# Two-layer decoder on one core: every head pair's probabilities turned by VectorE and four SBUF-to-SBUF transfers, with values and scores placed in six visits a layer

## The chip, the cores and the metric

The kernel runs on one core of one Trainium2 chip. The metric is the device time of one execution in microseconds. Three runs of the kernel before gave 641.29, 641.0 and 639.86 us, median 641.0. PE is TensorE (PEld its weight loads), DVE VectorE, ACT ScalarE, POOL GpSimd and SP SyncE; POOL and SP issue the transfers (DMAs), and "q" behind a name is the engine's queue of such issues.

## The reference, cut to what matters

One sequence of 256 rows, 1024 wide, passes two layers and a last RMSNorm, all in float32. Each layer is

```
u = rmsnorm(h);  q, k, v = heads(u @ w_in)         # 16 heads of 64
h = h + merge(softmax(q k^T / 8 + bias, causal) v) @ w_o
u = rmsnorm(h);  h = h + (silu(u @ w_g) * (u @ w_u)) @ w_out   # 2816 wide
h = h + sigmoid(rmsnorm(h) @ w_gate) * (p @ w_up)
```

In layer 0 the bias is that of the forgetting attention, a difference of running sums of log-sigmoids that are a small projection of u. Layer 1 is block-sparse attention with blocks of 256 keys; with 256 rows there is one block, so it comes down to causal attention with a learned bias by distance (T5 buckets).

## The kernel before, in words

**Matmuls.** Every large product is taken in three passes of 32-bit matmuls on values split into a high and a low part: high by high, high by low, low by high (`mm3`, L94, L95, L96). Weights come through SP's queue as 512 or 540 KB blocks (`raw`, 6 buffers), ACT makes the high part (`whi`) and DVE the low one (`wlo`), and PE goes through the blocks in order. PSUM is a ring of 8 banks.

**Attention.** The 16 heads are taken as 8 pairs (0 to 7). `project` makes q and k of a pair (tile `pq`), the score matmuls go to `sp` (L546, L549, and in layer 0 a bias product, L374), DVE adds the mask or bias and takes row minima into `e` (L563), ACT takes the exponential with its row sum (L567), and the reciprocal `rc` of the sums scales it. For the product with v the scaled probabilities must be turned, so that keys lie on the partitions (`pt`). The turn is made in three ways:

- **Pairs 0 to 4**: ACT scales (`scaled`, L600), DVE turns 32 by 32 blocks within each partition group (`turn`, L607, two STREAM_TRANSPOSE of 128x384), POOL writes the 384 KB to DRAM (L619, tile `dt`), and when that has landed reads it back in four DMAs of 96 KB (L622).
- **Pair 5**: the same, but with 16 DMAs of 24 KB from SBUF to SBUF in place of the trip to DRAM (L614), ten on POOL's queue and six on SP's.
- **Pairs 6 and 7**: DVE scales (`normal`, L591), TensorE turns in 12 transposes a layer (`transposes`, L637), ACT copies from PSUM (L644).

`values` then multiplies v with the turned probabilities (L654 and L656, tile `po`), and ACT and DVE split the result into the high and low parts of `o` (L287, L288). The output projection is cut into eight parts (`wo`, 24 matmuls each, parts 0 to 7), and part n can begin once its columns of `o` are there and its weights split.

**Order.** A scheduler puts each engine's instructions in an order, held to that of the code by `issue_after`, `held` and the entries of `marks`. After the last projection PE does in each layer: scores 5 and 6 with values 1 and 2; part 0; scores 7; parts 1 and 2; values 3 with the transposes of pairs 6 and 7; part 3; values 4 and 6, 5 and 7; parts 4, 5, 6; part 7. Between these, DVE and ACT do minima, exponentials, scaling, turns, the splits of `o` and the splits of the weights. Each of those stretches in plain 32-bit matmuls between the three-pass ones is called a visit below. The tiles `e` and `turn` share 4 buffers, `pt` has 3.

Of the kernel before, what the change touches and what calls it, by code (L numbers as in the profile page):

```python
# [27 lines left out]
F32 = mybir.dt.float32  # L28
# [24 lines left out]
TURNED = ((0, 1, 2, 3, 4, 5), (0, 1, 2, 3, 4, 5))  # L53
# [22 lines left out]
def trunk(ctx: ExitStack, tc: tile.TileContext, xg, wx, xr, pt, w, cst, gf, rel, hot, rvm, out):  # L76
# [352 lines left out]
    def attention(layer, nm, mid, early, nf):  # L429
# [50 lines left out]
        qk, sm = {}, {}  # L480
# [12 lines left out]
        def project(j, a):  # L493
# [16 lines left out]
            far = [x for x in fresh if x[0] in TURNED[layer]]  # L510
            near = [x for x in fresh if x[0] not in TURNED[layer]]
# [7 lines left out]
            for x in near:  # L519
                with tc.issue_after(got.ins):  # L520
                    got = normal(*x)
# [16 lines left out]
        def scores(*js, then=()):  # L538
# [16 lines left out]
            for n, j in enumerate(js):  # L555
# [9 lines left out]
                for s in range(2):  # L565
                    for q in range(2):
                        last = nc.scalar.activation(e[:, s, sl[q]], e[:, s, sl[q]], AF.Exp, scale=-1.0,  # L567
                                                    bias=mn[:, 0, s, q:q + 1], accum_out=mn[:, 1, s, q:q + 1])
# [17 lines left out]
        def normal(j, e, mn):  # L586

            rc = inverse(j, mn)
            for q, c in enumerate((slice(0, P), slice(P, 3 * P))):
                at = e[:, :, c]  # L590
                got = nc.vector.tensor_tensor(at, at, rc[:, :, q:q + 1].to_broadcast(list(at.shape)), op=ALU.mult)  # L591
            sm[j] = e
            return got

        def scaled(j, e, mn):

            rc = inverse(j, mn)
            for s in range(2):
                for q, c in enumerate((slice(0, P), slice(P, 3 * P))):
                    nc.scalar.activation(e[:, s, c], e[:, s, c], AF.Copy, scale=rc[:, s, q:q + 1])  # L600
            return rc

        def turn(j, e):

            t = work.tile([P, 4, 3, 2, 32], F32, tag="e", bufs=4, name=f"turn{layer}_{j}")
            for s in range(2):
                nc.vector.transpose(t[:, :, :, s].rearrange("p c b x -> p b c x"),  # L607
                                    e[:, s].rearrange("p (b c x) -> p b c x", b=3, x=32))
            if j == 5:
                p = work.tile([P, 4, 3, 2, 32], F32, tag="pt", bufs=3, name=f"pt{layer}_{j}")  # L610
                for n in range(16):
                    a, i = divmod(n, 4)
                    queue = nc.sync if n % 8 in (0, 3, 6) else nc.gpsimd
                    queue.dma_start(p[32 * i:32 * i + 32, a], t[32 * a:32 * a + 32, i])  # L614
                for s in range(2):
                    pts[2 * j + s] = p[:, :, :, s].rearrange("p c b x -> p b c x")
                return
            d = dram.tile([P, 6 * P], F32, name=f"dt{layer}_{j}")
            nc.gpsimd.dma_start(d, t.rearrange("p c b s x -> p (c b s x)"))  # L619
            p = work.tile([P, 4, 3, 2, 32], F32, tag="pt", bufs=3, name=f"pt{layer}_{j}")  # L620
            for i in range(4):
                nc.gpsimd.dma_start(p[32 * i:32 * i + 32].rearrange("p c b s x -> p c (b s x)"),  # L622
                                    bass.AP(tensor=d.tensor, offset=d.offset + 192 * i,
                                            ap=[[6 * P, 32], [32 * 6 * P, 4], [1, 192]]))
            for s in range(2):
                pts[2 * j + s] = p[:, :, :, s].rearrange("p c b x -> p b c x")

        pts = {}

        def transposes(j, tag="pt"):  # L630

            e = sm.pop(j)
            for s in range(2):
                i = 2 * j + s
                pp = bank(f"pp{layer}_{i}")
                for q in range(3):
                    got = nc.tensor.transpose(pp[:, q * P:(q + 1) * P], e[:, s, q * P:(q + 1) * P], ident)  # L637
                if tag == "pt":
                    if s == 0:
# [468 lines left out]
```

## Time and profile before

| | |
|---|---|
| median of three runs | 641.0 us |
| the runs | 641.29, 641.0, 639.86 us |
| span of the profiled execution, first to last instruction | 638.6 us |
| granted clock of TensorE | 0.998 |
| PE busy | 630.3 us, 99% of the span |
| DVE, ACT, POOL busy | 71%, 59%, 7% |
| DMA | 134.87 MB, mean 211 GB/s |
| attention's tail, layer 0 and layer 1 | about 78.8 to 102, 390.4 to 414 us |

The profiled execution's own time isn't given apart from its span; against the first run of the three, 641.29 us, the span leaves 2.7 us that lie before the first and behind the last instruction, against the median 2.4 us.

A row of the timeline has the start in us from the span's start, the time from the start of the first to the end of the last of the instructions merged in it, engine, line, operation, tiles written and read, shape and count; a bracket at its end tells how long the engine had been idle just before, and what ended that. Matmuls overlap, so the start of the next row is a better end for a row of them than its own length.

### The profile page before, as it was taken

How to read it: one execution, taken by the hardware profiler on the slowest of the kernel's cores; microseconds unless marked ns; L12 is line 12 of the kernel's file. 1: busy time of each engine (PE TensorE's matmuls, PEld its weight loads, DVE VectorE, ACT ScalarE, POOL GpSimd, SP SyncE). 2: the span in 40 equal slices, each digit the busy share in tenths (PEclk: the TensorE clock that was granted, in tenths of full speed). 3: DMA queues.
4: the chain of work that ended last, by engine and by line, in shares of the span. 5: the costliest groups of instructions: out<-in, count | busy, mean ns of one | idle time of the engine just before them, and what ended most of it. 6: DMA issues, size and time to landing. Idle time of an engine off the chain costs nothing.

```text
span 638.6 us, 13183 instructions
## 1 busy us (share of the span) xinstructions
PE 630.3 (99%) x5285; PEld 608.4 (95%) x5285; DVE 454.8 (71%) x738; ACT 379.3 (59%) x657; POOL 47.6 (7%) x93
## 2 busy tenths in 40 slices
PE   9999999999999999999999999999999999999995
PEld 7899999999999999999989999899999999999985
DVE  6777888776666666659892788888666666666685
ACT  6677787654444445448664689866444444454663
POOL 0102350000000000000000034300000000000001
PEclk9999999999999999999999999999999999999999
DMA  8846987497766666566674579756766666666523
GB/s 337 318 141 210 261 235 264 133 339 262 236 201 197 196 198 214 184 200 198 190 245 164 185 260 264 236 190 211 211 193 197 199 201 199 194 204 190 191 92 107
DMA packets 41469, 134.87 MB, mean 211 GB/s; under 512 B 5408, under 2 KB 10432, under 8 KB 41408
## 3 DMA queue, kind: packets, MB, share of 16 engines
q1 hardware_dynamic: 37616, 125.05, 60.9%
q0 software_dynamic: 3360, 8.36, 4.6%
q8 instruction: 41, 0.67, 0.4%
q10 hardware_dynamic: 432, 0.62, 0.3%
q14 instruction: 20, 0.16, 0.1%
HBM read 127.17 MB, written 9.20 MB: 214 GB/s over the span
## 4 chain that ended last, share of the span: by engine, by line
PE 95%; ACT 1%; DMA 1%; DVE 1%; issue 1%; POOL 0%; SPq 0%; POOLq 0%; DVEq 0%; ACTq 0%
PE gu L94 13%; PE gu L95 13%; PE gu L96 13%; PE fo L96 6%; PE fo L95 6%; PE fo L94 6%; PE pq L94 5%; PE pq L95 5%; PE pq L96 5%; PE v L425 4%; PE wo L94 2%; PE wo L96 2%; PE wo L95 2%; PE pg L94 2%; PE pg L95 2%; PE pg L96 2%
## 5 line engine op out<-in xcount | busy, mean ns | idle before, releaser
L168 DVE TENSOR_TENSOR wlo<-raw,whi 128x1024 fp32r<-128x1024 f32 (+1 forms) x166 | 200.8, 1216 | 76.4 <-ACT whi L166 70.7
L166 ACT ACTIVATE whi<-raw 128x1024 fp32r<-128x1024 f32 x164 | 171.9, 1058 | 104.6 <-issue 51.2
L94 PE MATMUL gu<-g,whi 128*128 128x256 f32 x704 | 194.9, 277 | 0.0
L95 PE MATMUL gu<-g,whi 128*128 128x256 f32 x704 | 194.7, 277 | 0.0
L96 PE MATMUL gu<-g,wlo 128*128 128x256 f32 x704 | 194.5, 276 | 0.0
L96 PEld LDWEIGHTS gu<-g,wlo 128*128 128x128 f32 x704 | 132.3, 188 | 0.0
L95 PEld LDWEIGHTS gu<-g,whi 128*128 128x128 f32 x704 | 132.2, 188 | 0.1
L94 PEld LDWEIGHTS gu<-g,whi 128*128 128x128 f32 x704 | 132.2, 188 | 0.0
L96 PE MATMUL fo<-fp,wlo 128*128 128x256 f32 x352 | 97.4, 277 | 0.0
L94 PE MATMUL fo<-fp,whi 128*128 128x256 f32 x352 | 97.3, 276 | 0.0
L95 PE MATMUL fo<-fp,whi 128*128 128x256 f32 x352 | 97.3, 276 | 0.0
L185 DVE TENSOR_TENSOR wlo<-raw,whi 128x1080 fp32r<-128x1080 f32 x40 | 50.9, 1279 | 29.5 <-ACT whi L184 28.9
L94 PE MATMUL pq<-g,whi 128*128 128x256 f32 x256 | 71.4, 279 | 0.0
L95 PE MATMUL pq<-g,whi 128*128 128x256 f32 x256 | 70.8, 276 | 0.0
L96 PE MATMUL pq<-g,wlo 128*128 128x256 f32 x256 | 70.8, 276 | 0.0
L95 PEld LDWEIGHTS fo<-fp,whi 128*128 128x128 f32 x352 | 66.2, 188 | 0.0
L94 PEld LDWEIGHTS fo<-fp,whi 128*128 128x128 f32 x352 | 66.1, 188 | 0.0
L96 PEld LDWEIGHTS fo<-fp,wlo 128*128 128x128 f32 x352 | 66.1, 188 | 0.0
L184 ACT ACTIVATE whi<-raw 128x1080 fp32r<-128x1080 f32 x40 | 43.7, 1101 | 27.6 <-PE gu L95 27.1
L94 PEld LDWEIGHTS pq<-g,whi 128*128 128x128 f32 x256 | 48.1, 188 | 0.9
L95 PEld LDWEIGHTS pq<-g,whi 128*128 128x128 f32 x256 | 48.1, 188 | 0.1
L96 PEld LDWEIGHTS pq<-g,wlo 128*128 128x128 f32 x256 | 48.1, 188 | 0.0
(189 smaller groups left out, 1023.8 us busy)
## 6 DMA issues: line engine op xcount, KB each, us to landing
raw<-w SPq DMA_DIRECT2D x173, 512.0 KB, 4.0
raw<-w SPq DMA_DIRECT2D x40, 540.0 KB, 4.0
dt<-turn POOLq DMA_DIRECT2D x10, 384.0 KB, 4.1
pt<-dt POOLq DMA_DIRECT2D x40, 96.0 KB, 5.5
d<-d SPq DMA_DIRECT2D x4, 768.0 KB, 6.4
bias<-d SPq DMA_DIRECT2D x4, 512.0 KB, 6.3
dh<-end SPq DMA_DIRECT2D x2, 512.0 KB, 2.6
ut<-dh SPq DMA_DIRECT2D x8, 128.0 KB, 3.0
```

The costliest lines, as they stand in the source:

```text
L94: mm(o, ah, bh, start=start, stop=False, skip_group_check=True)
L95: mm(o, ah, bl, start=False, stop=False, skip_group_check=True)
L96: return mm(o, al, bh, start=False, stop=stop, skip_group_check=True)
L166: state["hi"] = state[f"hi{i}"] = nc.scalar.activation(hi[:, c], raw[:, c], AF.Copy)
L168: nc.vector.tensor_tensor(lo[:, c], raw[:, c], f32(hi[:, c]), op=ALU.subtract)
L184: nc.scalar.activation(ht, raw[:, 0:WW], AF.Copy)
L185: state["lo"] = nc.vector.tensor_tensor(lt, raw[:, 0:WW], f32(ht), op=ALU.subtract)
L425: got = mm(bks[2 * t + hf], x[a][:, t * P:(t + 1) * P], w[b][:, hf * HC:(hf + 1) * HC], start=k + a + b == 0, stop=k + b == KT, skip_group ...
```

## The change

`TURNED`, the trip to DRAM, the 16 small DMAs, `transposes` and its copies go. All eight pairs are turned by `turn`: DVE's two STREAM_TRANSPOSE now read `e` with a stride of four elements (in 32-element runs that take every fourth key), so that a 32-partition group of the result holds, for one group of 32 queries, all 128 keys of a block, and four DMAs of 96 KB each take such a group from SBUF to its place in `pt` in SBUF. Their destination is 128 partitions by 192 elements, 768 bytes in a run. For pairs 0 to 4 all four are on POOL's queue; for pairs 5, 6 and 7 two are on POOL's and two on SP's. `pt` has 5 buffers. Pair 6 is now scaled by ACT; pair 7 still by DVE (`normal`), and then turned. The values of pair 3 and the scores of pair 7 join the first visit, and the order after the projections is: scores 5 and 6, values 1, 2 and 3, scores 7; parts 0, 1, 2; values 4 and 5; parts 3, 4; values 6 and 7; parts 5, 6; part 7. The scratch that POOL's queue keeps its descriptors in is set to 8192 bytes of a partition.

```diff
-                if j < NP - 3:
+                if j < NP - 3 or j == NP - 1:
                     fresh.append((j, e, mn))
-                elif j in TURNED[layer]:
+                else:
                     scaled(j, e, mn)
                     fresh.append((j, e))
-                else:
-                    marks[-j] = last, normal(j, e, mn)
...
         def turn(j, e):
             t = work.tile([P, 4, 3, 2, 32], F32, tag="e", bufs=4, name=f"turn{layer}_{j}")
             for s in range(2):
-                nc.vector.transpose(t[:, :, :, s].rearrange("p c b x -> p b c x"),
-                                    e[:, s].rearrange("p (b c x) -> p b c x", b=3, x=32))
-            if j == 5:
...
-            d = dram.tile([P, 6 * P], F32, name=f"dt{layer}_{j}")
-            nc.gpsimd.dma_start(d, t.rearrange("p c b s x -> p (c b s x)"))
-            p = work.tile([P, 4, 3, 2, 32], F32, tag="pt", bufs=3, name=f"pt{layer}_{j}")
-            for i in range(4):
-                nc.gpsimd.dma_start(p[32 * i:32 * i + 32].rearrange("p c b s x -> p c (b s x)"),
-                                    bass.AP(tensor=d.tensor, offset=d.offset + 192 * i,
-                                            ap=[[6 * P, 32], [32 * 6 * P, 4], [1, 192]]))
+                got = nc.vector.transpose(t[:, :, :, s].rearrange("p c b x -> p b c x"),
+                                          e[:, s].rearrange("p (b y c) -> p b c y", b=3, c=4))
+            p = work.tile([P, 4, 3, 2, 32], F32, tag="pt", bufs=5, name=f"pt{layer}_{j}")
+            for a in range(4):
+                queue = nc.sync if j > 4 and a % 2 else nc.gpsimd
+                queue.dma_start(p[:, a].rearrange("p b s x -> p (b s x)"),
+                                t[32 * a:32 * a + 32].rearrange("p c b s x -> p (c b s x)"))
...
-            got = scores(*range(max(j - 1, 0), min(j + 1, NP - 1)), then=(1, 2) if j == 6 else ())
+            got = scores(*range(max(j - 1, 0), min(j + 1, NP - 1)), then=(1, 2, 3) if j == 6 else ())
...
+        with tc.issue_after(got.ins):
+            got = scores(NP - 1)
+        marks["mid"] = marks[7][0], marks["low"]
         got = behind(got, 6, 0)
         fetch(1, "t")
+        with tc.issue_after(state["lo"].ins):
+            turn(*fresh.pop(0))
         fetch(2, "mid")
+        turn(*fresh.pop(0))
+        fetch(3, "mid")
+        x = fresh.pop(0)
+        normal(*x)
+        marks["third"] = (turn(*x[:2]),)
+        got = behind(got, "t", 1)
         got = behind(got, "mid", 2)
         with tc.issue_after(got.ins):
-            values(3)
-            marks["third"] = marks["o"]
-            transposes(NP - 2, "fp")
-            got = transposes(NP - 1, "fp" if far else "pt")
-        got = behind(got, -6, 3)
+            got = values(4, 5)
+            marks["o4"] = marks["o"]
+        got = behind(got, "mid", 3)
+        got = behind(got, "third", 4)
         with tc.issue_after(got.ins):
-            values(4, 6 if far else 5)
-            got = values(5 if far else 6, 7)
-        got = behind(got, "third", 4)
-        behind(got, "third", 5, 6)
+            got = values(6, 7)
+        behind(got, "o4", 5, 6)
...
-    nc = bacc.Bacc("TRN2", target_bir_lowering=False, num_devices=1)
+    nc = bacc.Bacc("TRN2", target_bir_lowering=False, num_devices=1, dynamic_dma_scratch_size=8192)
```

Three places show how the order moves. In the names a number behind the pair's is the tile's own (`po_3_1106` is `po` of pair 3); `sp_14` and `sp_15` are the two heads of pair 7. The lines are those of the kernel that the rows come from.

The first is PE's first visit of layer 0, behind scores 5 and 6. Before:

```order
L654 MATMUL po_1_1114<-pt_1_791,v 64x256 x2
L654 MATMUL po_2_1115<-pt_2_801,v 64x256 x2
L656 MATMUL po_1_1114<-pt_1_791,v 64x128 x2
L656 MATMUL po_2_1115<-pt_2_801,v 64x128 x2
L94 MATMUL wo_0_0_1158<-o_369,whi_1163 128x256
```

Now:

```order
L616 MATMUL po_1_1104<-pt_1_787,v 64x256 x2
L616 MATMUL po_2_1105<-pt_2_795,v 64x256 x2
L616 MATMUL po_3_1106<-pt_3_1000,v 64x256 x2
L618 MATMUL po_1_1104<-pt_1_787,v 64x128 x2
L618 MATMUL po_2_1105<-pt_2_795,v 64x128 x2
L618 MATMUL po_3_1106<-pt_3_1000,v 64x128 x2
L373 MATMUL sp_14_1161<-c,sel 128x384
```

PE reads `pt` of pair 3 before it does any part of the output projection, where before it came three parts later; scores 7 stand right behind.

The second is POOL's row of DMA issues in layer 0. Before:

```order
L619 DMA dt_3_1006<-turn_3_1003 128x768
L619 DMA dt_4_1016<-turn_4_1013 128x768
L622 DMA pt_3_1008<-dt_3_1006 32x4x192 x4
L622 DMA pt_4_1018<-dt_4_1016 32x4x192 x4
L614 DMA pt_5_1207<-turn_5_1204 32x192 x10
```

Now:

```order
L602 DMA pt_3_1000<-turn_3_997 128x1x192 x4
L602 DMA pt_4_1008<-turn_4_1005 128x1x192 x4
L602 DMA pt_5_1222<-turn_5_1219 128x1x192 x2
L602 DMA pt_6_1236<-turn_6_1233 128x1x192 x2
L602 DMA pt_7_1254<-turn_7_1251 128x1x192 x2
```

One step from `turn` to `pt` where there were two, each with its own landing.

The third is DVE's tail in layer 1, from the first half of pair 5's turn to that of pair 7 (`wlo_5158` and `wlo_5172` are the low weights of parts 2 and 3):

```order
L597 STREAM_TRANSPOSE turn_5_5148<-e_5_5055 128x3x4x32
L184 TENSOR_TENSOR wlo_5158<-raw_5156,whi_5157 128x1080
L576 RECIPROCAL rc_6_5081<-mn_6_5072 128x4
L597 STREAM_TRANSPOSE turn_5_5148<-e_5_5055 128x3x4x32
L184 TENSOR_TENSOR wlo_5172<-raw_5170,whi_5171 128x1080
L597 STREAM_TRANSPOSE turn_6_5162<-e_6_5071 128x3x4x32 x2
L576 RECIPROCAL rc_7_5176<-mn_7_5102 128x4
L584 TENSOR_TENSOR e_7_5101<-e_7_5101,rc_7_5176 128x2x128
L584 TENSOR_TENSOR e_7_5101<-e_7_5101,rc_7_5176 128x2x256
L597 STREAM_TRANSPOSE turn_7_5180<-e_7_5101 128x3x4x32 x2
```

Before, the two halves of pair 5's turn stood together behind part 2's low weights, and there was none for pairs 6 and 7. Now part 2's low weights stand between the halves of pair 5's turn. On SP's queue the two DMAs of `pt_5` stand behind the issue of the weights `raw_5440`.

More of the change, by code (lines that the diff above doesn't have):

```diff
@@ L479, in attention @@
         oh, ol = o[:, :, 0], o[:, :, 1]
-        qk, sm = {}, {}
+        qk = {}
         pq = {}
@@ L509, in project @@
             del pq[j]
-            far = [x for x in fresh if x[0] in TURNED[layer]]
-            near = [x for x in fresh if x[0] not in TURNED[layer]]
+            far = fresh[:]
             fresh.clear()
@@ L518, in project @@
             marks["t"] = marks.get(j - 1, (got,))[0], got
-            for x in near:
-                with tc.issue_after(got.ins):
-                    got = normal(*x)
             th = work.tile([P, 3 * P], F32R, tag="qkh", bufs=3, name=f"qkh{layer}_{j}")
@@ L590, in normal @@
                 at = e[:, :, c]
-                got = nc.vector.tensor_tensor(at, at, rc[:, :, q:q + 1].to_broadcast(list(at.shape)), op=ALU.mult)
-            sm[j] = e
-            return got
+                nc.vector.tensor_tensor(at, at, rc[:, :, q:q + 1].to_broadcast(list(at.shape)), op=ALU.mult)
         def scaled(j, e, mn):
@@ L628, in attention @@
+            return got
         pts = {}
[L630 to L639, printed above, removed]
-                        both = work.tile([P, 2, 3 * P], F32, tag="pt", bufs=3, name=f"pt{layer}_{j}")
-                    t = both[:, s]
-                else:
-                    t = work.tile([P, 2 * S], F32, tag="fp", bufs=4, name=f"pt{layer}_{i}")[:, 0:3 * P]
-                nc.scalar.activation(t, pp[:, 0:3 * P], AF.Copy)
-                pts[i] = t.rearrange("p (b c x) -> p b c x", b=3, x=32)
-            return got
@@ L692, in behind @@
             return got
+        with tc.issue_after(got.ins):
+            got = scores(NP - 1)
+        marks["mid"] = marks[7][0], marks["low"]
         got = behind(got, 6, 0)
-        far = 5 in TURNED[layer]
-        marks["mid"] = marks[7][0], marks["low"] if far else marks[-5][1]
         fetch(1, "t")
+        with tc.issue_after(state["lo"].ins):
+            turn(*fresh.pop(0))
         fetch(2, "mid")
-        if far:
-            with tc.issue_after(state["lo"].ins):
-                turn(*fresh.pop())
-        with tc.issue_after(got.ins):
-            end = scores(NP - 1)
-        got = behind(end, "t", 1)
-        if not far:
-            with tc.issue_after(got.ins):
-                got = transposes(5, "fp")
+        turn(*fresh.pop(0))
[4 more added lines that the diff above has]
+        got = behind(got, "t", 1)
         got = behind(got, "mid", 2)
         with tc.issue_after(got.ins):
-            values(3)
-            marks["third"] = marks["o"]
-            transposes(NP - 2, "fp")
-            got = transposes(NP - 1, "fp" if far else "pt")
-        got = behind(got, -6, 3)
+            got = values(4, 5)
+            marks["o4"] = marks["o"]
+        got = behind(got, "mid", 3)
+        got = behind(got, "third", 4)
         with tc.issue_after(got.ins):
-            values(4, 6 if far else 5)
-            got = values(5 if far else 6, 7)
-        got = behind(got, "third", 4)
-        behind(got, "third", 5, 6)
+            got = values(6, 7)
+        behind(got, "o4", 5, 6)
         state["o"] = marks["o"]
@@ L722, in attention @@
             if hf:
-                wo(7, "third")
+                wo(7, "o4")
             for b in range(2):
```

16 lines of the change are left out of this document (3 added, 13 removed).

## The prediction

> **What bounds the kernel now.** I read the page first, then the list of what PE waited for, then the timelines of PE, POOL, DVE and ACT in the tail of attention in each layer, since the diff touches nothing else.
>
> ```profile
> span 638.6 us, 13183 instructions
> PE 630.3 (99%) x5285; PEld 608.4 (95%) x5285; DVE 454.8 (71%) x738; ACT 379.3 (59%) x657; POOL 47.6 (7%) x93
> PE cold L111 <- PEq L1100: 0.8, 1, 0.8
> PE po L654 <- ACT o L287: 0.6, 1, 0.6
> ```
>
> PE is busy for 99% of the span and the list of its waits has two entries, 0.8 us at the start and 0.6 us at the end of layer 1's attention. So time is gained only by taking work from PE or that one wait, and every new wait of PE is paid in full. DVE, ACT and POOL matter only where they make PE wait.
>
> **What leaves PE.** The rows of layer 0's tail, then of layer 1's:
>
> ```profile
> 84.69 0.28 PE L95 MATMUL wo<-o,whi 128*128 128x256 f32 x1
> 84.81 0.28 PE L96 MATMUL wo<-o,wlo 128*128 128x256 f32 x1
> 85.02 0.44 PE L374 MATMUL sp<-c,sel 64*128 64x384 f32 x2
> ...
> 85.97 0.39 PE L94 MATMUL wo<-o,whi 128*128 128x256 f32 x1
> 86.19 0.28 PE L95 MATMUL wo<-o,whi 128*128 128x256 f32 x1
> ...
> 91.65 0.65 PE L654 MATMUL po<-pt,v 128*64 128x256 f32 x4
> 92.13 0.39 PE L656 MATMUL po<-pt,v 128*64 128x128 f32 x4
> 92.45 1.56 PE L637 MATMUL pp<-con,e 128*128 128x128 f32 x12
> 93.77 0.37 PE L94 MATMUL wo<-o,whi 128*128 128x256 f32 x1
> ```
>
> ```profile
> 402.60 0.65 PE L654 MATMUL po<-pt,v 128*64 128x256 f32 x4
> 403.09 0.39 PE L656 MATMUL po<-pt,v 128*64 128x128 f32 x4
> 403.40 1.56 PE L637 MATMUL pp<-con,e 128*128 128x128 f32 x12
> 404.72 0.37 PE L94 MATMUL wo<-o,whi 128*128 128x256 f32 x1
> ...
> 409.72 1.08 PE L654 MATMUL po<-pt,v 128*64 128x256 f32 x8 [0.56 <-ACT o L287]
> ```
>
> The 12 transposes take 93.77 - 92.45 = 1.32 us, and 404.72 - 403.40 = 1.32 in layer 1: 2.64 together. Three-pass matmuls follow each other every 0.12 us (84.69 to 84.81). Into a visit the step is 85.02 - 84.81 = 0.21, out of it 86.19 - 85.97 = 0.22, so each visit costs about 0.2 beside its contents. Behind the projections a layer has four visits now and three after the change: 0.2 a layer, 0.4 together. The 0.56 us wait of layer 1 stands in the middle of a visit of four pairs, for the copies of the two before; the change splits it in two of two pairs with two parts between, so I let it go. Saved: 2.64 + 0.4 + 0.56 = 3.6 us.
>
> **What is late next: pair 3.** PE now wants `pt` of pair 3 in the first visit. When it wants it, and when the turned pair was ready:
>
> ```profile
> 80.55 1.08 PE L654 MATMUL po<-pt,v 128*64 128x256 f32 x8
> 81.46 0.61 PE L656 MATMUL po<-pt,v 128*64 128x128 f32 x8
> 82.00 0.38 PE L94 MATMUL wo<-o,whi 128*128 128x256 f32 x1
> 392.65 0.61 PE L656 MATMUL po<-pt,v 128*64 128x128 f32 x8
> 393.19 0.39 PE L94 MATMUL wo<-o,whi 128*128 128x256 f32 x1
> ```
>
> ```profile
> 76.12 1.95 DVE L607 STREAM_TRANSPOSE turn<-e 128x384 f32<-128x384 f32 x4
> 77.44 0.56 POOL L619 DMA_DIRECT2D dt<-turn  x1 [6.08 <-DVE turn L607]
> 81.78 2.21 POOL L622 DMA_DIRECT2D pt<-dt  x4 [2.86 <-DMA dt<-turn]
> 389.68 0.56 POOL L619 DMA_DIRECT2D dt<-turn  x1 [5.06 <-DVE turn L607]
> ```
>
> The third pair's first matmuls take the place in which L656 begins now: 81.46 in layer 0, 392.65 in layer 1. POOL begins the first transfer of pair 3 at 77.44 and 389.68; one issue takes 2.21 / 4 = 0.55, so the fourth begins 1.65 later, at 79.09 and 391.33. PE waits if that one lands more than 2.37 us (81.46 - 79.09) behind its issue in layer 0, more than 1.32 in layer 1. No transfer of 96 KB from SBUF to SBUF is in the trace. The nearest rows are POOL's reads of 96 KB from DRAM. The first pair of lines is those issued from 397 to 398 us, the second those from 81.7 to 83.6:
>
> ```profile
> L622 POOL DMA_DIRECT2D pt<-dt x3: 550/552/552, 396.5 to 397.6; - x3
> DMA to landing us min/median/max: 2.5/2.8/3.7
> ...
> DMA to landing us min/median/max: 5.7/5.8/6.2
> ```
>
> ```profile
> 79.24 2.06 SPq L151 DMA_DIRECT2D raw<-w  x2
> 391.48 2.17 SPq L151 DMA_DIRECT2D raw<-w  x2
> ```
>
> The slow ones were issued behind two 512 KB weight blocks (79.24 and the next); the quick ones had none issued beside them for 3 us. Pair 3's four transfers are nearer to the quick: the next weight blocks are issued at 79.24 and 391.48, each just behind the fourth. I take the quick rows' median, 2.8, and keep 2.5 and 5.8 for the range. In layer 0 the wait is 79.09 + 2.8 - 81.46 = 0.43 us, in layer 1 391.33 + 2.8 - 392.65 = 1.48.
>
> [...]
>
> **What is late after that: pair 5 in layer 1.** Its chain runs over ACT's scaling, DVE's turn and, between the two halves of the turn, part 2's low weights:
>
> ```profile
> 390.10 1.04 ACT L136 ACTIVATE whi<-raw 128x1024 fp32r<-128x1024 f32 x1
> 394.92 0.64 ACT L287 ACTIVATE o<-po 128x256 fp32r<-128x256 f32 x2
> 397.20 1.49 ACT L600 ACTIVATE e<-e,rc 128x128 f32<-128x128 f32 x4
> 396.87 1.28 DVE L185 TENSOR_TENSOR wlo<-raw,whi 128x1080 fp32r<-128x1080 f32 x1
> 398.06 1.24 DVE L607 STREAM_TRANSPOSE turn<-e 128x384 f32<-128x384 f32 x2
> ```
>
> ACT now has one high weight more ahead of this scaling (about 1.0) and the split of pair 3's `o` (0.64 / 2 = 0.32), so it begins near 397.20 + 1.3 = 398.5, and its first half is done 0.7 later, at 399.2. DVE then takes 1.95 / 4 = 0.49 for a half turn, 398.06 - 396.87 = 1.19 for the low weights, 0.49 for the other half: 401.4. POOL and SP begin 0.25 later and each issues its second after 0.55: 402.2. Transfers of this place, 24 KB each, and PE's parts:
>
> ```profile
> L614 SPq DMA_DIRECT2D pt<-turn x5: 533/584/593, 399.4 to 401.9; - x5
> DMA to landing us min/median/max: 3.3/3.8/4.4
> ...
> 395.92 0.28 PE L96 MATMUL wo<-o,wlo 128*128 128x256 f32 x1
> 396.12 0.49 PE L546 MATMUL sp<-qkt 64*128 64x128 f32 x4
> 396.90 0.39 PE L94 MATMUL wo<-o,whi 128*128 128x256 f32 x1
> ```
>
> At 3.8 us pair 5 lands at 406.0. PE, undisturbed, would want it at 393.19 + 0.80 (values 3, 402.60 to 403.40) + 0.78 (scores 7, 396.12 to 396.90) + 8.39 (three parts of 395.92 - 393.19 = 2.73, and 0.2 for the visit) + 0.45 (half the 0.91 of eight L654) = 403.6; with the 1.48 of pair 3, 405.1. I count 0.9 us, between nothing (landing in 2.5: 404.7) and 1.5 (in 4.4: 406.6 less 405.1).
>
> **What stays hidden.** Pair 5 in layer 0: ACT's scaling there starts 1.3 later too, and both half turns stand together; that gives 92.7 for the landing against 93.0 for PE. A landing 0.6 us later would cost 0.3. Pair 7: its turn uses the buffer of pair 5's, so DVE waits until that has landed (406.0); 1.0 for the turn, 0.8 to the second issue and 3.8 bring 411.6, where PE, by 1.45 for the visit of two pairs (80.55 to 82.00) and two parts, wants it at 403.6 + 1.45 + 5.7 + 2.4 of waits = 413.1. Behind that waiting turn stand the low weights of part 4, wanted at the same time or later; the cover is 1.5 us and goes if pair 5 lands later than that. DVE's share of new work is two turns (1.95) less one `normal`, about 1.0 a layer; ACT gains 1.5 of scaling and loses four copies. They are paid from idle time:
>
> ```profile
> sum 63.00, PE 62.44 PEld 57.63 DVE 53.70 ACT 51.69 POOL 20.89; mean PE 31.22 PEld 28.82 DVE 26.85 ACT 25.84 POOL 10.44
> ```
>
> In the two tails together (73 to 105, 385 to 416 us) DVE is idle for 9.3 us and ACT for 11.3. The smaller descriptor scratch changes nothing that a row shows; I cost it at nothing.
>
> **The sum.** -3.6 + 0.43 + 1.48 + 0.9 = -0.8 us, so a span of 637.8. The profiled span leaves 2.4 us to the median of the runs, 641.0; with the same 2.4 I expect 640.2 us. About half of the saving of layer 0 stays, and layer 1 gives its own back: 1.32 + 0.2 + 0.56 = 2.1 against 2.4 of waits.
>
> **Rivals.**
>
> *The transfers land fast.* With 2.5 us, the quickest 96 KB row, the waits are 0.13 + 1.18 and pair 5 is hidden: -3.6 + 1.3 = -2.3, or 638.7 us. For it: nothing of the weights is issued while pair 3's transfers are, and both their ends lie in SBUF. Against it: the whole 384 KB of pair 3 took 3.7 us to land in layer 0 and 4.1 in layer 1, as the views of `dt` give it:
>
> ```profile
> DMA to landing us min/median/max: 3.7/3.7/3.7
> DMA to landing us min/median/max: 4.1/4.1/4.1
> ```
>
> Less the 1.65 of the three earlier issues that leaves 2.1 and 2.4 for the same bytes, so layer 0's would allow it and layer 1's be nearer to it than to my 2.8.
>
> *The strided turn runs at half rate.* DVE now reads every fourth element. No row of this kernel shows such a read. Doubling a half turn adds 0.49, a pair's turn 0.97. Pair 3 would be ready 0.97 later in both layers and PE would wait so much longer; pair 5's chain moves by as much as PE, so its term stays. -0.8 + 1.9 = +1.1: 642.1 us. [...] Against it: the turn now moves 384 elements a partition in 0.49 us, 1.3 ns an element, a pace at which a read may still keep up.
>
> *Slower than before: the transfers queue with the weights.* If the fourth one shares the DMA engines with the 512 KB issued 0.15 us behind it, it lands in 4 to 5.8 us, as the POOL reads from 81.78 on did. At 4.8: 79.09 + 4.8 - 81.46 = 2.4 and 3.5, pair 5 then hidden behind the longer wait: -3.6 + 5.9 = +2.3, or 643.3 us. This decides from a landing of about 3.7 us on, where the two waits, 1.33 and 2.37, take back the saving. For it: the four reads of the same size from the same queue; against it: those were issued behind the weights, these ahead.
>
> **How the numbers follow.** My forecast, 640.2, has a chance of 0.45 (landing between 2.6 and 3.7 us, 639.2 to 641.8), the fast landing 0.24, the half-rate turn 0.12, the queueing 0.19. A measurement of this kernel tells 0.2%, about 1.3 us, from no change: 639.7 and 642.3 are the bounds. Faster takes the fast landing and a third of the forecast: 0.39. Within: the other two thirds and half of the half-rate case, 0.37. Slower: the queueing and the other half, 0.24. The range goes from 638.0 (the fast landing's 638.7, less the 0.13 + 0.5 that a landing half a microsecond quicker than any row would save) to 643.3, the queueing's middle.
>
> **What would show it.** In the profile after: no L637; PE's list of waits with `po` released by DMA `pt<-turn`, about 0.4 us near 81.5 and 1.5 near 392.7 (right), none (fast landing), over 2 each (queueing); a third such wait of some 0.9 near 405. The group of STREAM_TRANSPOSE with a mean near 538 ns (right) or near 1000 (half rate). The landing of `pt<-turn` in the table of issues, 2.8 (right), 2.5 or less, over 4. I am wrong if PE waits for weights or for PSUM in the tail, which nothing here foresees.

## The result and the profile after

The changed kernel takes 648.4 us (median of four runs, 647.9 to 648.8). Its ratio to the kernel before is 1.0118, with an interval from 1.0105 to 1.0132: it is slower by 1.2%, where 640.2 was forecast and the range ended at 643.3. The span of the profiled execution grew from 638.6 to 646.1 us, by 7.5. One execution of a later experiment, c_mid3, took 787.7 us at a granted clock of 0.85 and is not in its ratio; without it the median given there, 643.97, is 643.6.

From the page of the changed kernel: the busy times. Then what PE waited for in attention, where the same list had one entry of 0.6 us before:

```profile
PE 632.5 (98%) x5261; PEld 610.1 (94%) x5261; DVE 465.2 (72%) x742; ACT 378.5 (59%) x657; POOL 38.3 (6%) x75
```

```profile
PE po L616 <- DMA pt<-turn: 5.5, 2, 3.5
```

Two things stand out. The two waits of the forecast are there, at the right place and from the right releaser, and nothing else there waits; but they have 5.5 us, not 1.9. And PE executes 24 matmuls fewer than before, yet its busy time rose by 2.2 us (630.3 to 632.5).

The time can be put in a ledger by layer. The first and the last row of each layer's tail of attention, from the first scores behind the projections to the first `gu` matmul, in PE's timeline before:

```profile
78.84 0.44 PE L374 MATMUL sp<-c,sel 64*128 64x384 f32 x2
110.48 0.28 PE L94 MATMUL gu<-g,whi 128*128 128x256 f32 x1
390.38 0.49 PE L546 MATMUL sp<-qkt 64*128 64x128 f32 x3
422.18 0.28 PE L94 MATMUL gu<-g,whi 128*128 128x256 f32 x1
```

and after:

```profile
78.94 0.44 PE L373 MATMUL sp<-c,sel 64*128 64x384 f32 x2
112.89 0.28 PE L93 MATMUL gu<-g,whi 128*128 128x256 f32 x1
392.80 0.38 PE L541 MATMUL sp<-qkt 64*128 64x128 f32 x2
429.24 0.28 PE L93 MATMUL gu<-g,whi 128*128 128x256 f32 x1
```

Layer 0's tail went from 31.64 to 33.95 us, layer 1's from 31.80 to 36.44: +2.31 and +4.64, together 6.95 of the 7.5. What happened in them starts in the first visit. PE's timeline of the changed kernel, layer 0 and layer 1:

```profile
80.64 1.08 PE L616 MATMUL po<-pt,v 128*64 128x256 f32 x8
83.71 0.92 PE L616 MATMUL po<-pt,v 128*64 128x256 f32 x4 [1.99 <-DMA pt<-turn]
84.35 1.56 PE L618 MATMUL po<-pt,v 128*64 128x128 f32 x12
87.48 0.39 PE L93 MATMUL wo<-o,whi 128*128 128x256 f32 x1
...
394.16 1.08 PE L616 MATMUL po<-pt,v 128*64 128x256 f32 x8
398.77 1.12 PE L616 MATMUL po<-pt,v 128*64 128x256 f32 x4 [3.53 <-DMA pt<-turn]
412.05 0.44 PE L616 MATMUL po<-pt,v 128*64 128x256 f32 x2
```

The values of pairs 1 and 2 take 0.91 us from step to step (80.55 to 81.46 in the rows of before), so those of pair 3 could have begun at 81.55 and 395.07. They begin 2.16 and 3.70 us later: 5.9 us. Then the matmuls behind the wait are slow: the twelve of L618 take 1.56 us, and the same twelve take 0.85 in a_contig below. The reason stands in the column of the granted clock. The views of stretches of 1 us, of the changed kernel; the columns are the stretch, its length, busy time of PE, PEld, DVE, ACT and POOL, the granted clock, the share of the DMA engines, GB/s:

```profile
83.00:84.00 1.00, 0.29 (x4) 0.28 (x6) 1.00 (x3) 1.00 (x2) 0.80 (x2) 0.98 0.92 165
84.00:85.00 1.00, 1.00 (x11) 0.88 (x9) 1.00 (x8) 1.00 (x2) 0.00 (x0) 0.50 0.87 347
...
87.00:88.00 1.00, 1.00 (x10) 0.82 (x9) 0.99 (x3) 1.00 (x4) 0.00 (x0) 0.81 0.32 129
...
397.00:398.00 1.00, 0.00 (x0) 0.00 (x0) 1.00 (x3) 0.52 (x2) 1.00 (x3) 0.99 0.80 198
398.00:399.00 1.00, 0.23 (x2) 0.26 (x4) 1.00 (x2) 1.00 (x3) 0.81 (x2) 0.50 1.06 191
...
404.00:405.00 1.00, 1.00 (x7) 1.00 (x7) 0.88 (x4) 1.00 (x5) 0.00 (x0) 0.59 0.00 0
```

Half the clock is granted from 84 to about 87.4 and from 398 to about 404.8. It also explains why PE is busier with less work. Its price is found beside two of the experiments below, which do the same matmuls at full clock: 83.71 to 87.48 is 3.77 us here and 2.18 in a_contig, so 1.6; 398.77 to 412.05 is 13.28 here and 10.46 in c_light, so 2.8. The ledger of the tails is then: waits 5.9, half clock 4.4, and what is left, 6.95 - 5.9 - 4.4 = -3.3, is the work saved. Of the rest of the 7.5, about 0.1 us lies ahead of layer 0's tail and 0.45 behind layer 1's.

Why is pair 3 late? The pieces of the chain of waits of the changed kernel (start, length, what), in layer 0 and in layer 1:

```profile
77.54 1.65 DVE turn L597 x2
...
79.47 1.37 POOL pt L602 x3
...
81.06 2.52 DMA pt<-turn
...
394.48 1.37 POOL pt L602 x3
...
396.06 2.52 DMA pt<-turn
```

The last of the four transfers, the unknown of the forecast, took 2.52 us, quicker than the 2.8 taken. But POOL begins at 79.47 and 394.48 instead of 77.44 and 389.68. Against the first values of the visit (80.55 and 391.74 before, the latter 0.91 ahead of the 392.65 of L656; 80.64 and 394.16 now) that is 1.94 us and 2.38 us later. The group of the turn, before and after (count, busy us, mean ns):

```profile
L607 DVE STREAM_TRANSPOSE turn<-e 128x384 f32<-128x384 f32 x24 | 12.2, 551 | 0.2
```

```profile
L597 DVE STREAM_TRANSPOSE turn<-e 128x384 f32<-128x384 f32 x32 | 26.0, 862 | 0.2
```

A half turn that reads every fourth element takes 862 ns, 1.6 times the 551 of before, 0.31 us more, and from one start to the next 0.82 instead of 0.49. Pair 3's own two halves account for 0.6 of the delay. The rest was there already when its turn began, at 77.54 instead of 76.12, 1.4 us later: six half turns of pairs 0 to 2 stand ahead of it in the layer, and at 0.31 us each they make 1.9. DVE was idle at times in the projections. Most of that is one entry in its list of waits from 48 to 78 us, here of the changed kernel,

```profile
DVE qkl L523 <- ACT qkh L521: 3.5, 5, 1.1
```

which is the time that ACT needs to answer DVE's own instruction before. It is 3.5 us in the kernel before as well: a DVE that comes later asks later, so this idle time takes nothing of the delay away. Only one wait for PE (0.35 us behind the first pair's turn in the timeline of before) was used up.

### The profile page after: what moved, and what is told of

Read it like the earlier page. It is cut to its first block, busy times and chain, and to the rows that moved or that the text cites. A ratio compares the mean times of both kernels' runs of the same rounds, so it can differ in the third digit from the quotient of the medians.

```text
span 646.1 us, 13133 instructions
## 1 busy us (share of the span) xinstructions
PE 632.5 (98%) x5261; PEld 610.1 (94%) x5261; DVE 465.2 (72%) x742; ACT 378.5 (59%) x657; POOL 38.3 (6%) x75
## 4 chain that ended last, share of the span: by engine, by line
PE 84%; ACT 5%; DVE 5%; issue 2%; DMA 2%; POOL 1%; SPq 0%; DVEq 0%; POOLq 0%; ACTq 0%
PE gu L93 12%; PE gu L94 12%; PE gu L95 12%; PE fo L95 6%; PE fo L94 6%; PE fo L93 6%; PE v L424 4%; PE wo L93 3%; ACT e L562 2%; PE wo L94 2%; PE wo L95 2%; DVE turn L597 2%; PE pg L93 2%; PE pg L94 1%; PE pg L95 1%
```

## The experiments

Each ran beside the kernel before on the same chip, and each ratio is to that. The suspects are the strided turn (theory 1 in the expectations), the early place of pair 3's values (2), the half clock behind a wait (3), and the transfers of pair 3 beside the weights (4). Where the turn reads contiguously, `pt` holds the keys in another order than `v`, so the products are other numbers of the same shape and work.

**The change with a contiguous turn** (a_contig).

```
-  e[:, s].rearrange("p (b y c) -> p b c y", b=3, c=4)
+  e[:, s].rearrange("p (b c x) -> p b c x", b=3, x=32)
```

> The changed kernel, with the turn reading in order again (no stride of four elements), all else as changed. The keys of a block then reach TensorE in another order than v's rows, so the attention's values are other numbers; the work and its order are the same. Theory 1 (the strided read makes VectorE late, and through it TensorE): a half turn falls from 0.79 to 0.48 us apart, the wait for pair 3 from 1.99 to about 0.1 us in layer 0 and from 3.53 to about 1.1 us in layer 1, no wait for pair 5 or under 1 us in layer 1: 638.5 to 640.5 us. Theory 2 (pair 3 is wanted too early, whatever the turn takes): both waits stay over 1.5 us, 645 us or more.

646.97 us, ratio 1.0091 [1.0075, 1.0106]. The turn is back at 0.55 us a half, and POOL begins where the prediction had it, but almost nothing is won. Pieces of its chain in layer 0, then SP's row of weight issues, and the same row of the changed kernel:

```profile
76.05 1.04 DVE turn L597 x2
...
77.37 1.37 POOL pt L602 x3
...
78.95 5.03 DMA pt<-turn
```

```profile
79.17 2.06 SPq L150 DMA_DIRECT2D raw<-w  x2
```

```profile
81.84 2.06 SPq L150 DMA_DIRECT2D raw<-w  x2
```

The transfers, 2.1 us earlier in issue, land later: at 83.98, where the strided kernel's landed at 81.06 + 2.52 = 83.58. Two weight blocks of 512 KB are issued from 0.2 us behind the last transfer on, where the strided kernel issued them 0.8 behind. In layer 1, with the weights again just behind, the last took 4.7. So the stride is a cause, but not the only one. PE's visit shows the price at full clock, since here layer 0 keeps it:

```profile
84.12 0.65 PE L616 MATMUL po<-pt,v 128*64 128x256 f32 x4 [2.53 <-DMA pt<-turn]
...
86.30 0.39 PE L93 MATMUL wo<-o,whi 128*128 128x256 f32 x1
```

That is the 2.18 us of the ledger. Layer 1 waited 3.4 us and had half the clock again. So both waits stayed over 1.5 us, as theory 2 said, and the times of theory 1 did not come.

**The change with pair 3's values in the second visit** (a_late), the strided turn kept.

```
-  then=(1, 2, 3) if j == 6
+  then=(1, 2) if j == 6
...
-  got = values(4, 5)
+  got = values(3, 4, 5)
```

> The changed kernel with its strided turn, but the values of pair 3 taken from the first visit and put into the second, with those of pairs 4 and 5. Theory 2 (only the early place of pair 3 is wrong): no wait is left, 648.4 less 5.5 of waits and 5.4 of slow matmuls behind them, 637.5 us. Theory 1 (VectorE is late for everything): the wait moves to the second visit, where pair 5 lands about 2.4 us late in layer 0 and 3 to 4 in layer 1: 644 to 648 us.

649.11 us, ratio 1.0123 [1.0107, 1.014]: as slow as the change, and far from the 637.5 of theory 2. The first entries of PE's list of waits:

```profile
PE sp L541 <- DVE qkt L514: 1.8, 1, 1.8
PE wo L94 <- DVE o L287: 1.7, 2, 1.4
```

The wait for `pt` is gone from the first visit, and PE waits instead for the queries and keys of pair 7 (1.4 us more for `qkl`), the splits of `o` and the low weights, all of them DVE's; the wait for pair 5 that theory 1 had is only 0.5 us. Layer 1 ran at half clock from 401.1 to 404.5. With values 3 out of the way scores 7 come earlier, so this run moved two things. It does show that DVE is late in other work there, not in the turn alone.

**The kernel before with the strided read** (b_stride): nothing but that line.

```
-  e[:, s].rearrange("p (b c x) -> p b c x", b=3, x=32)
+  e[:, s].rearrange("p (b y c) -> p b c y", b=3, c=4)
```

> The kernel before, with nothing changed but the read of the turn, strided as in the change; the keys reach TensorE in another order than v's rows, so the attention's values are other numbers. Theory 1: VectorE is 1.4 us late at pair 3's turn in layer 0 and 2 us at pair 5's, and more in layer 1, which pair 7's scaling hands on to the transposes: a wait of TensorE of 1 to 3 us in each layer, 643 to 648 us. Theory 2 (the stride is harmless, the place of pair 3 is what costs): 641 us as before.

646.8 us, ratio 1.0095 [1.008, 1.011]. Without the new order, the new transfers or the new turns, the stride costs the kernel before some 6 us, within what theory 1 gave. Its turn in layer 0, which began at 76.12 and took 1.95 us for four halves before, and its first wait of PE:

```profile
77.61 3.16 DVE L607 STREAM_TRANSPOSE turn<-e 128x384 f32<-128x384 f32 x4
```

```profile
PE wo L94 <- DVE mn L563: 2.2, 2, 1.2
```

The clock stayed at 1.00 in both tails, so none of it is half clock. The list names 3.3 us more than before; the rest of the 6.2 in span is not explained.

**The kernel before with the new path** (b_path): pairs 0 to 5 go by four transfers from SBUF to SBUF, contiguous turn, old order.

```
-  nc.gpsimd.dma_start(d, t.rearrange("p c b s x -> p (c b s x)"))
-  for i in range(4): nc.gpsimd.dma_start(p[32 * i:32 * i + 32]..., <d, 192 * i>)
+  for a in range(4):
+      queue = nc.sync if j > 4 and a % 2 else nc.gpsimd
+      queue.dma_start(p[:, a]..., t[32 * a:32 * a + 32]...)
```

> The kernel before with one part of the change alone: pairs 0 to 5 go from the turn, which reads in order, to their place by four transfers within SBUF, no trip to DRAM; order, TensorE's transposes of pairs 6 and 7 and ScalarE's copies as before. The values of these pairs are other numbers, since the keys reach TensorE in another order. Theory 6 (the transfers themselves cost TensorE nothing where nothing waits for them early): 640 to 642 us, no wait of TensorE beyond the 0.6 us of before. Rival (the transfers disturb the weights or the engines): waits for weights, 643 us or more.

640.46 us, ratio 0.9997 [0.9987, 1.0006]. The one new wait is 0.2 us. The path alone costs nothing and brings nothing in the old order, where `pt` is read later.

**Pair 3's odd transfers on SP's queue** (c_sp, with the contiguous turn).

```
-  queue = nc.sync if j > 4 and a % 2 else nc.gpsimd
+  queue = nc.sync if j not in (0, 1, 2, 4) and a % 2 else nc.gpsimd
```

> The kernel a_contig (the changed one with the turn reading in order, values in another key order), with two of pair 3's four transfers on SP's queue, as pairs 5 to 7 have it, so that the last is issued about 1.1 us earlier, ahead of the weight block that SP issues at 79.17 us. Theory 4 (the transfers of pair 3 are slow only where they share the DMA engines with a 512 KB weight block): all four land within 2.6 us of their issue, no wait for pair 3 in layer 0, under 0.6 us in layer 1, 637.5 to 640 us. Rival (four SBUF-to-SBUF transfers in a row are slow in themselves, or while VectorE works): the last still lands over 3.7 us behind its issue, waits over 1 us, 643 us or more.

643.67 us, ratio 1.0043 [1.0028, 1.0058], with two waits left:

```profile
82.62 0.65 PE L616 MATMUL po<-pt,v 128*64 128x256 f32 x4 [1.05 <-DMA pt<-turn]
395.08 0.65 PE L616 MATMUL po<-pt,v 128*64 128x256 f32 x4 [1.98 <-DMA pt<-turn]
```

Two queues issue the four sooner, and SP's two stand ahead of the weights; it wins nearly half of a_contig's loss. But they did not land within 2.6 us, as theory 4 had it. SP's second, issued at 77.79 and 390.40, 1.4 us ahead of the weights, still took 4.70 and 4.55 us, over the 3.7 of the rival, and the time is the rival's too:

```profile
77.79 4.70 DMA pt<-turn
```

So the distance to the weights doesn't decide by itself how long a transfer takes. Layer 1's wait of 1.98 us still halved the clock, from 396.2 to 399.6.

**The weight block beside pair 3's transfers cut to a sixteenth** (c_light, contiguous turn). In each layer one block of 512 KB is loaded only in its first 64 columns and split from these repeated; the rest of its values are left out.

```
+  n = 64 if i in (30, 138) else c.stop
+  state["row"] = queue.dma_start(raw[:, c.start:n], w[max(i - 2, 0)][:, c.start:n])
```

> The kernel a_contig with 15/16 of one weight block left out in each layer (32 KB in place of 512 KB, its matmuls use those numbers again): the block that SP issues 0.2 us behind pair 3's fourth transfer, at 79.2 us and in layer 1 at 393.3. Theory 4 (that block is what makes pair 3's transfers land after 3.7 to 5.0 us): all four land within 2.7 us, the wait falls from 2.53 to 0.2 us or none in layer 0 and from 3.37 to about 1 in layer 1. Rival (they are slow among themselves, eight transfers of 96 KB in a row): the last still lands over 3.7 us behind its issue and the wait stays over 1.5 us in layer 0.

641.62 us (eight runs), ratio 1.0017 [1.0006, 1.0027]. Against the kernel before in their own sessions c_light loses 641.62 - 640.73 = 0.89 us and a_contig 646.97 - 641.22 = 5.75, so one block in each layer was worth 4.9 of the 5.75, the half clock of a_contig's layer 1 included. PE's timeline:

```profile
83.42 0.65 PE L623 MATMUL po<-pt,v 128*64 128x256 f32 x4 [0.98 <-DMA pt<-turn]
395.11 0.65 PE L623 MATMUL po<-pt,v 128*64 128x256 f32 x4 [1.23 <-DMA pt<-turn]
405.57 0.44 PE L623 MATMUL po<-pt,v 128*64 128x256 f32 x2
407.21 0.65 PE L623 MATMUL po<-pt,v 128*64 128x256 f32 x4 [0.99 <-DMA pt<-turn]
```

In layer 1 the last transfer of pair 3 now lands in 2.6 us, not 4.7, and the wait is near the 1 of theory 4. In layer 0 it lands in 3.48, not 5.03, and the wait of 0.98 lies between theory 4 and its rival. The other block of 512 KB, issued at 81.75, does not account for that: the second of the four, issued at 78.8, takes 3.9 us in this kernel as in a_contig, and it would have landed before 81.75 at the 2.5 us of layer 1. What slows layer 0's transfers beside the block that was cut stays open. The clock stayed at 1.00, and 395.11 to 405.57 is the 10.46 us of the ledger. Of all runs this one is nearest to the change as it was forecast, with a contiguous turn, landings of 3.48 and 2.6 us against 2.8, and pair 5 waiting in layer 1, and even it is no faster than the kernel before.

**Pair 3's values and scores 7 one part later** (c_mid, contiguous turn).

```
-  then=(1, 2, 3) if j == 6
+  then=(1, 2) if j == 6
...
+  got = behind(got, 6, 0)
-  got = scores(NP - 1)
+  got = scores(NP - 1, then=(3,))
-  got = behind(got, 6, 0)
```

> The kernel a_contig with pair 3's values and pair 7's scores taken one part of the output projection later (scores 5 and 6, values 1 and 2; part 0; scores 7 and values 3; parts 1, 2 and on as changed): one visit more a layer, 0.2 us each. Pair 3 is wanted 2.9 us later. Theory 5 (all that is wrong, once the turn reads in order, is that pair 3 is wanted before its transfers can be there): no wait in layer 0, under 1 us in layer 1, the granted clock stays at 1.0, 638 to 640.5 us. Rival (pairs 5 to 7 are late as well, by ScalarE's and VectorE's longer tail): waits of over 1 us move to the later visits, 642 us or more.

643.81 us, ratio 1.005 [1.0033, 1.0067], as the rival had it. PE no longer waits for pair 3, but for others:

```profile
PE wo L95 <- DVE wlo L184: 2.6, 2, 1.6
...
PE po L616 <- DMA pt<-turn: 0.7, 1, 0.7
```

Two kernels then let the low weights go earlier: **c_mid2** those of parts 2 and 3, **c_mid3** those of part 2 alone.

```
+  marks["mid"] = marks[7][0], marks["low"]     (c_mid2: set before scores 7)
```

```
+  marks["two"] = marks[7][0], marks["low"]     (c_mid3: set before scores 7)
-  fetch(2, "mid")
+  fetch(2, "two")
```

> The kernel c_mid (turn in order; pair 3's values and pair 7's scores one part later) with the low weights of parts 2 and 3 no longer held back until pair 7's minima: VectorE does them in the time in which c_mid has it idle (84.3 to 88.2 us). If the waits that are left in c_mid (2.6 us for low weights, 0.7 for pair 5) are an order on VectorE and no lack of time, the first go and 638.5 to 640.5 us come out. If VectorE and ScalarE have too much to do in the tail, the waits move to pair 5 or 7: 641.5 to 644 us.

> The kernel c_mid (turn in order, values in another key order; pair 3's values and pair 7's scores one part later) with part 2's low weights alone taken from behind pair 5's turn, part 3's left there. Theory 7 (what is left over in c_mid and c_mid2 is one order on VectorE, either weights or pair 5 first): no wait of over 0.5 us in the two tails, the 3.0 us that the transposes and the removed wait of layer 1 are worth are seen, 638 to 639.5 us. Rival (with TensorE 3 us quicker the tail is bound by VectorE, ScalarE and the transfers together, and a wait is only moved): waits of 2 us or more again, at pair 5 or at part 3's weights, 640.5 to 643 us.

644.28 us, ratio 1.0053 [1.0036, 1.0071], and 643.97 us, 1.005 [1.0033, 1.0068]: no gain from either, and both a little above what even the rivals gave. The longest wait in c_mid3:

```profile
PE po L616 <- DMA pt<-turn: 2.3, 1, 2.3
```

The wait for low weights became two for pair 5, this one in layer 1 and one of 1.5 for its turn in layer 0, where the turn now stands behind those low weights on DVE; c_mid2 has the same two (1.9 and 1.4) in its profiled execution, which at 642.04 us is the fastest of its six. In these three kernels the place of the wait was chosen, and the sum did not get smaller (3.3, 3.3 and 4.1 us).

**c_mid2's order with the strided turn** (s_mid2), the whole computation in one of these orders.

> The same order as c_mid2, but with the strided turn of the change, so that all of the computation is done. Theory 1 (the strided read makes VectorE 1.4 us late at pair 3's turn in layer 0 and 0.3 more with each turn's half): 2 to 4 us above c_mid2, 641 to 645 us. Rival (in this order VectorE has the time): within 1 us of c_mid2.

650.46 us, ratio 1.017 [1.0144, 1.0196], 6 us behind c_mid2, where theory 1 had 2 to 4. That is as much as the stride costs in b_stride, but here a part of it is half clock, from 413.6 to 417.0.

**The stride moved elsewhere.** The keys have to be interleaved by someone. In **a_wr** DVE's minimum writes the scores in the turned order, and in **x6_mid3** (c_mid3's order) ACT scales into another buffer in that order; the turn then reads contiguously, in a_wr in two pieces a half.

```
+  nc.vector.tensor_tensor_reduce(e[:, s, sl[q]].rearrange("p (c m) -> p m c", c=4), ...)      (a_wr)
```

```
+  nc.scalar.activation(x[:, s, c].rearrange("p (b c y) -> p b y c", c=4, y=32), ...)         (x6_mid3)
```

> The changed kernel with the stride moved: VectorE writes the scores' differences in the order that the turn needs (a stride in its output), and the turn reads in order; all of the computation is done. If a strided write costs VectorE nothing, it is a_contig: 645.5 to 647.5 us, minima at 0.28 and 0.42 us as before. If it costs as a strided read does (1.6 times), the minima take 0.45 and 0.68 and the chain behind them is late: 648 us or more.

> The order of c_mid3 with all of the computation done and no stride on VectorE: ScalarE's scaling of every pair, pair 7's too, writes a second tile in the order that the turn needs (6 buffers shared by e, the scaled tile and turn, 4 for pt, 7168 bytes of descriptors). If ScalarE writes with a stride at its usual pace (0.39 and 0.49 us for 128 and 256 columns), VectorE is on time as in c_mid3 and pair 7's scaling is moved from VectorE: within 1.5 us of c_mid3, at or under 641 us. If the strided write costs ScalarE as it costs VectorE (1.4 to 1.6 times), its scaling takes 0.6 us more a pair and 643 us or more come out.

647.91 us, ratio 1.0101 [1.0068, 1.0134], and 652.77 us, 1.0184 [1.0167, 1.0201]. The groups by shape, DVE's minimum before and in a_wr:

```profile
L563 DVE CUSTOM_DVE_ANT_0 e<-sp,con 128x256 f32<-128x256 f32 x16 | 6.7, 418 | 0.0
```

```profile
L558 DVE CUSTOM_DVE_ANT_0 e<-sp,con 128x256 f32<-128x256 f32 x16 | 10.0, 626 | 0.0
```

and ACT's scaling before and in x6_mid3:

```profile
L600 ACT ACTIVATE e<-e,rc 128x256 f32<-128x256 f32 x24 | 11.9, 497 | 0.0
```

```profile
L593 ACT ACTIVATE x<-e,rc 128x256 f32<-128x256 f32 x32 | 23.7, 742 | 0.0
```

The strided write cost each of the two engines 1.5 times the contiguous one, 626 ns against 418 and 742 against 497. Neither engine took the interleaving for nothing, and PE still waits for `pt`, 4.8 us in a_wr and 6.9 in x6_mid3, with half clock at both waits in each. x6_mid3 also moves other work, so its time is not the price of the write alone.

**Filling the wait** (a_fill, a_fill2): the change itself, with dummy matmuls between pair 2 and pair 3 to keep PE busy, so that only the clock differs.

```
+  if js == (1, 2, 3) and i == 4:
+      for _ in range(FILL[layer]): mm(po[d, :S], v[...], ...)      (a_fill: 17, 30; a_fill2: 5, 8)
```

> The changed kernel with 17 (layer 0) and 30 (layer 1) more matmuls ahead of those of pair 3 in the first visit, on pair 2's operands and into the bank that pair 3's overwrite: 1.95 and 3.45 us of work at 0.115 us each in the place of the wait. Theory 3 (the lower granted clock behind the wait costs 1.9 and 3.6 us beyond the wait itself): the granted clock stays near 1.0 in both tails, 643 us. Rival (the matmuls behind the wait are slow because VectorE and ScalarE are then at work on the same memory): they stay slow, 648 us.

> The changed kernel with 5 (layer 0) and 8 (layer 1) more pairs of matmuls ahead of those of pair 3 in the first visit, at the 0.43 us apiece that a_fill showed: 2.1 and 3.4 us of work in the place of the waits of 1.99 and 3.53. Theory 3 (the half clock behind the waits costs 1.9 and 3.6 us by itself): granted clock 1.0 in both tails, 642.5 to 644 us. Rival (the matmuls behind are slow for another reason): 648 us.

a_fill overshot: 659.3 us, ratio 1.0291 [1.0275, 1.0306], since a dummy (two matmuls) took 0.43 us and not the 0.115 assumed, so the fill lasted 7 and 13 us. a_fill2 took 651.3 us, 1.0163 [1.0148, 1.0178]. Its visit in layer 0, and its first wait of PE:

```profile
81.46 2.32 PE L619 MATMUL po<-pt,v 128*64 128x256 f32 x10
83.75 0.65 PE L621 MATMUL po<-pt,v 128*64 128x256 f32 x4
...
84.99 0.45 PE L374 MATMUL sp<-c,sel 64*128 64x384 f32 x2
```

```profile
PE wo L94 <- DVE o L288: 3.4, 2, 2.0
```

Pair 3 begins at the same time as in the change (83.75 against 83.71) and the clock stays at 1.00 in both tails, where it falls to 0.50 behind the change's 1.99 and 3.53 us of idle time, so it is PE's idle time that takes the clock, as theory 3 said. But PE, 0.9 us sooner at scores 7 (84.99, where the change has 85.84), now waits for DVE, and ACT's order had shifted too (the splits of `o` behind pair 5's scaling), so the time does not isolate the price of the half clock: I expected this kernel to be quicker than the change, and it is 2.9 us slower.

## Why the prediction was wrong

**What leaves PE: right, but for one term.** Without waits and half clock the tails are 3.3 us shorter by the ledger, against 3.6. The twelve transposes and layer 1's wait make 2.64 + 0.56 = 3.2 of that; the four tenths for fewer visits came to 0.1 or so. Part of why is in the rows of layer 0: the last visits of two pairs take 1.45 and 1.56 us after (95.89 to 97.34, 103.05 to 104.61), where the one of four pairs took 2.75 before (96.69 to 99.44), so splitting it cost 0.26.

**"What is late next: pair 3": the right wait, priced by the wrong term. This step failed first.** The whole uncertainty went into the landing, 2.8 us with 2.5 and 5.8 as bounds, and the landing came out at 2.52. The start of the issue, 77.44 and 389.68, was copied from the trace of before as if fixed. It moved by 1.94 and 2.38 us against PE, because DVE was slower, and 0.43 and 1.48 became 2.16 and 3.70.

**The half-rate rival saw the cause and under-priced it.** I charged it 0.97 us a layer, for pair 3's own two halves, at twice the pace. The pace is 1.6 times. What I missed is that the turns of pairs 0 to 2 stand ahead of it on DVE in the projections, where most of DVE's idle time is time that it waits for ACT's answers, so that 0.31 us a half adds up: 1.3 us of the 1.94 in layer 0 were owed before pair 3's turn began (77.54 against 76.12, less the 0.1 by which PE was later itself). b_stride, where nothing but the stride changes, begins this turn at 77.61, and a_contig, without the stride, at 76.05. b_stride gives the whole bill, 6 us on the kernel before, where the rival, with a chance of 0.12, had +1.9. No run shows the doubled half turn that this rival's sum took: DVE's strided read took 1.6 times as long as the contiguous one (862 ns against 551), DVE's strided write 1.5 times (626 against 418 in a_wr) and ACT's 1.5 times (742 against 497 in x6_mid3). My argument against this rival, that 1.3 ns an element may leave room, was wrong.

**The queueing rival was right about the change without its stride.** With the transfers at the predicted 77.4, a_contig shows the last landing in 5.0 us with the weights issued 0.2 behind it, inside that rival's 4 to 5.8, and c_light takes 4.9 of the 5.75 us away with one block a layer. In the change itself the transfers and the weights behind them are later, and the four land in 2.2 to 2.7. So the late start with the stride and the slow landing without it make PE wait about equally long, 5.5 and 5.9 us in its lists, and removing the stride brings the other; that is why a_contig is only some 1.5 us faster than the change. That the weights make the landing slow is shown for layer 1; in layer 0 the cut block took away 1.55 us, and why c_sp's took 4.70 with the weights 1.4 us behind stays open.

**The clock was in no term. This step failed second.** "Every new wait of PE is paid in full" counted a wait once. It was paid 1.75 times: 5.9 us of waits and 4.4 us at half pace behind them. The half pace is seen directly, as a granted clock of 0.50, its 4.4 us by comparison with two other kernels; a_fill2, which kept the clock in the change itself, did not isolate it.

When the clock fell can be worked out from the traces. In the three kernels that lose it in both layers, views of 0.05 us put the two drops at 83.96 and 397.99 (the change), 83.50 and 397.53 (a_wr), 96.06 and 416.91 (x6_mid3). They are 314.03, 314.03 and 320.85 us apart, which is 92, 92 and 94 times 3.413, and the stretches at half clock last 3.41 or 6.83 us, once or twice that. So in these three traces the clock changed at the ends of windows of 3.41 us, on one grid in both tails. In the change's trace a third drop at 643.75, after PE's last matmul, lies on it too: it is 559.79 us behind the first, 164 times 3.413. With such windows laid from the drops over the tails of the seven kernels that lost the clock there (these three, a_contig, c_sp, a_late, s_mid2), PE was idle for 1.89 us or more in each of the ten windows at whose end the clock was lost, and for at most 1.38 in those through which it was kept. It came back behind a window with 0.05 us of idle time or less, and not behind those with 0.78 or more. This is why the 1.99 us of the change, all in one window, lost the clock, and the 2.53 of a_contig's layer 0 did not: a window ends at 82.74, in the middle of that wait, and leaves 1.15 us on one side and 1.38 on the other. PE need not have been idle for all of a window: 1.89 us of idle time in 3.41 were enough.

**Pair 5.** The 0.9 us in layer 1 did not appear: the longer wait for pair 3 and the half clock came ahead of it, much as the queueing rival supposed. In c_light, where PE waits 1.2 us for pair 3, it is there with 0.99, near the 0.9.

**The expected gain.** Even with the stride and most of the slow landing away (c_light) the tails give back what they save: from step to step its three waits are 1.2 (82.26 to 83.42), 1.4 (393.71 to 395.11) and 1.2 us (405.57 to 407.21, less 0.45), 3.7 against the 3.3. c_mid, c_mid2 and c_mid3 move the waits from pair 3 to low weights to pair 5 without lowering their sum. Why the sum stays is not shown. DVE and ACT are not full there: in the two tails before they were busy for 53.70 and 51.69 us of 63, PE for 62.44. No kernel of the study was faster than the one before. Whether an order exists that spreads DVE's turns further into the projections stays open.

## What to carry to other kernels

Before an operand's layout is changed so that an engine reads it strided, take the engine's idle time in the stretch ahead of the place where its result is needed, and leave out the time in which it waits for an answer to its own work: what is left is all that can take up the extra time of the earlier instructions, and the rest arrives at that place together. When the busiest engine is relieved of work, look for the place where its new input comes from a chain of other engines and transfers, and date the whole chain in the new kernel, not from the old trace. A wait of the matmul engine can cost more than itself: in the change 4.4 us at half clock came behind 5.9 us of waits, three quarters as much again. In these runs it depended on how the wait lay to the windows: 1.99 us in one window lost the clock, 2.53 us shared by two did not.

## What the runs showed of the hardware

- A STREAM_TRANSPOSE of 128x384 fp32 that reads every fourth element took 862 ns in the change, where the contiguous one took 551 in the kernel before.
- DVE's minimum of 128x256 writing in strides took 626 ns in a_wr, where it took 418 contiguously in the kernel before, and ACT's scaling of 128x256 742 in x6_mid3 instead of 497.
- The same 96 KB transfer from SBUF to SBUF took 2.5 us in the change with the weights issued 0.8 us behind it (81.06 and 81.84), and 5.0 in a_contig with the weights 0.2 us behind (78.95 and 79.17). On SP's queue in c_sp it took 4.70 with the weights 1.4 us behind (77.79 and 79.16), so this distance isn't a rule.
- In the seven kernels that lost it in the tails, the granted clock fell to 0.50 behind windows of 3.41 us with 1.89 us or more of idle time of PE, and held through those with up to 1.38. A wait of 1.99 us in one window lost it (the change), and one of 2.53 that two windows shared did not (a_contig).
- The dummy matmuls of one pair's head, in a row, started every 0.23 us in a_fill2 (ten in 2.3 us), where matmuls that alternate between the two heads of a pair started every 0.11 (eight in 0.91).
